# One encoder layer on one core: the column blocks of the input projection in another order

## The chip, the cores and the metric

One core of a Trainium2 chip runs the kernel. The metric is the device time of one execution in microseconds: 886.13 us, median of three runs (884.5 to 888.79). Float32 products are made of three matmuls each: every operand is split into a rounded high part (hi) and a remainder (lo), and hi x hi, hi x lo and lo x hi are summed in PSUM.

## The reference

The input is 2048 tokens of 1024 features. After a LayerNorm one projection gives the columns of three mixers, whose gated outputs are joined and projected back:

```
x = layer_norm(x)
au, av, ag, ba, bb, bg, cq, ck, cv, cg = split(x @ w_in)      # 256,256,256 | 256,256,256 | 512,128,128,512
ya = gelu(au) * (w_s mixed over chunks of 128 tokens of layer_norm(gelu(av)) + b_s) * silu(ag)
yb = silu(layer_norm(depthwise_conv31(ba * sigmoid(bb)) + conv_b)) * silu(bg)
yc = window_attention(cq, ck, cv; +-128 tokens, bias, sink) * silu(cg)
y  = concat(ya, yb, yc) @ w_out
out = layer_norm(alpha * x + y)
```

## The kernel before

The tokens are 16 tiles of 128, in four chunks (NC = 4) of 512. The kernel has three phases. First, x is normalised and transposed into four tiles xc0 to xc3 (one for each chunk, 1024 features by 512 tokens, hi and lo), and the columns av, ck and cv are projected. Second, eighteen blocks of 128 columns are projected, one chunk at a time: 72 steps. A list named plan gives the blocks' order; ft_n_c in the rows is block n of the plan and chunk c. A step is `feat` (24 matmuls into a PSUM tile ft, L139 to L141) and `evac`, which takes the tile away by the kind of the column. Third, block by block of 128 tokens, come scores, softmax, transposes of p, the product with v, the gate and the output projection (`slot`); the first of these slots are put among the last eight steps, from tail0 = 64 on, by a table.

What `evac` does: a conv input bb goes through a sigmoid on ScalarE into glu, and ba is multiplied with it on VectorE (L461). A gMLP column au goes through gelu on ScalarE (L466), then VectorE multiplies it with the spatially mixed tile spT (L468); the matching ag goes through silu (L475), GpSimd multiplies (L478), and `store_y` makes a cast on ScalarE (L433), a remainder on GpSimd (L434) and two stores. A query block cq is split into hi (ScalarE) and lo (VectorE, L232) and stored. A conv gate bg is silu, a GpSimd product and `store_y`; an attention gate cg is silu and one store. ScalarE loads a table (ACT_TABLE_LOAD) when it turns between gelu, silu and exp.

Around these steps hang other pieces of work, tied to step numbers by `at(s, ...)`: the depthwise convolution, 62 operations over 2048 tokens on VectorE ("taps": L382 for the first of each half, L386 for the rest), of which `conv_step` issues so many per step; `vln_tile`, the gMLP's LayerNorm; `conv_ln_tile` and `conv_back`, the conv's LayerNorm with its transposes cl (L407) and cb (L424), two tiles per step from cl0 = 48; and `split_wo`, which loads a piece of w_out, splits it with a ScalarE cast and a GpSimd subtraction (L555) and stores both halves, since there is no room to keep them.

PSUM tiles come from four pairs of buffers, psA, psB, psD and psE. A step's tile is in psD; in psE for every other step of kinds cq and cg. psA holds spT, the transposes of p and, here, cl; psB the transposes cb and the product with v; psD also the scores; psE also the output projection. SyncE issues all DMAs in the order of its queue, and each engine works through its own queue in order. A scheduler chooses how the engines' instructions interleave, so an engine's order is not the order of the code.

Of the kernel before, what the change touches and what calls it, by code (L numbers as in the profile page):

```python
# [7 lines left out]
F32 = mybir.dt.float32  # L8
# [6 lines left out]
P = 128  # L15
# [5 lines left out]
NC = SEQ // CH  # L21
# [15 lines left out]
AU, AV, AG = 0, 256, 512  # L37
BA, BB, BG = 768, 1024, 1280
CQ, CK, CV, CG = 1536, 2048, 2176, 2304
# [16 lines left out]
def trunk_kernel(  # L56
# [42 lines left out]
    psp = tc.alloc_tile_pool(name="psp", bufs=2, space=PSUM)  # L99
# [3 lines left out]
    def rstd_of(pool, var, tag, scale=1.0):  # L103
        ve = pool.tile([P, 1], F32, tag=tag + "e", name=tag + "e", bufs=3)
        G.tensor_scalar(out=ve, in0=var, scalar1=scale, scalar2=EPS, op0=ALU.mult, op1=ALU.add)  # L105
        rs = pool.tile([P, 1], F32, tag=tag + "r", name=tag + "r", bufs=3)
        G.tensor_tensor(out=rs, in0=ve, in1=nhalf, op=ALU.pow)
        return rs

    def stats(pool, srcs, tag, stag=None):  # L110
        stag = stag or tag + "s"
        st = pool.tile([P, len(srcs), 6], F32, tag=stag, name=stag, bufs=2)
        for j, s in enumerate(srcs):
            V.bn_stats(out=st[:, j, :], in_=s)
        mv = pool.tile([P, 2], F32, tag=tag + "m", name=tag + "m", bufs=3)
        V.bn_aggr(out=mv, in_=st)  # L116
        return mv
# [16 lines left out]
    def feat(w, c, name, o=0, n=CH, tag="psD"):  # L134
        ps = psp.tile([P, n], F32, tag=tag, name="ft_" + name)
        hi, lo = w
        for k in range(NK):
            xh, xl = xc[c][:, 0, k, o:o + n], xc[c][:, 1, k, o:o + n]
            T.matmul(ps, hi[:, k, :], xh, start=(k == 0), stop=False)  # L139
            T.matmul(ps, hi[:, k, :], xl, start=False, stop=False)  # L140
            T.matmul(ps, lo[:, k, :], xh, start=False, stop=(k == NK - 1))  # L141
        return ps
# [22 lines left out]
    ps = psp.tile([NH, 512], F32, tag="psE", name="ps_tb")  # L165
# [96 lines left out]
    for t in range(NT + LOOK):  # L262
# [25 lines left out]
        if u >= 2 * TPC and u % TPC == 3:  # L288
# [1 line left out]
    keys(NC - 1, 0, CH)  # L290
    values(NC - 1, 0, CH)

    plan = [(BB, "bb", 0), (BA, "ba", 0), (BB + P, "bb", 1), (BA + P, "ba", 1),
            (AU, "au", 0), (AG, "ag", 0), (AU + P, "au", 1), (AG + P, "ag", 1)]
    plan += [(CQ + a * P, "cq", a) for a in range(4)]
    plan += [(CG + a * P, "cg", a) for a in range(2)]
    plan += [(BG + a * P, "bg", a) for a in range(2)]
    plan += [(CG + a * P, "cg", a) for a in range(2, 4)]
    wts = {}

    def want(n):
        if n < len(plan) and n not in wts:
            wts[n] = prep_w(plan[n][0], f"f{n}")
# [30 lines left out]
    def prep_spatial():  # L334
        SY.dma_start(vgb[:, 0, :], gmlp_ln_g[0].partition_broadcast(P))
        SY.dma_start(vgb[:, 1, :], gmlp_ln_b[0].partition_broadcast(P))
        wsr = pm.tile([P, 4, P], F32, tag="tmp", name="wsr")
        SY.dma_start(wsr, w_spatial[0].rearrange("h i j -> i h j"))
        SY.dma_start(bsp, b_spatial[0].rearrange("h i -> i h"))
        ps = psp.tile([P, 4 * P], F32, tag="psE", name="ps_wt")  # L340
        for h in range(4):
            T.transpose(ps[:, h * P:(h + 1) * P], wsr[:, h, :], ident)
        S.copy(wth, ps)
        V.tensor_tensor(out=wtl, in0=ps, in1=f32(wth), op=ALU.subtract)
# [17 lines left out]
    def spatial(g):  # L362
        vh, vl = vsp.pop(g)
        so = [pm.tile([P, 2, 256], F32, tag="tmp", name=f"so{g}_{j}") for j in range(2)]
        for h in range(4):
            ps = psp.tile([P, TPC, HD], F32, tag="psE", name=f"sp{g}_{h}")
            fs = slice(h * HD, (h + 1) * HD)
            cs = slice(h * P, (h + 1) * P)
            T.matmul(ps, wth[:, cs], vh[:, :, fs], start=True, stop=False)
            T.matmul(ps, wth[:, cs], vl[:, :, fs], start=False, stop=False)  # L370
            T.matmul(ps, wtl[:, cs], vh[:, :, fs], start=False, stop=True)
            for j in range(2):
                S.activation(so[j][:, :, fs], ps[:, 2 * j:2 * j + 2, :], AF.Identity, bias=bsp[:, h:h + 1])
        for j in range(2):
            r0 = (g * TPC + 2 * j) * P
            SY.dma_start(spo_d[r0:r0 + 2 * P, :].rearrange("(c p) f -> p c f", p=P), so[j])
# [17 lines left out]
    def conv_step(n):  # L394
        for _ in range(n):
            if avail[0] <= 0:
                return
            avail[0] -= 1
            next(conv)
# [2 lines left out]
    pbs = {}  # L402

    def conv_ln_tile(t):
        ps = psp.tile([P, 256], F32, tag="psA", name=f"cl{t}")
        for a in range(2):
            T.transpose(ps[:, a * P:(a + 1) * P], acc[a][:, t * P:(t + 1) * P], ident)  # L407
        mv = stats(pm, [ps], "ns")
        rs = rstd_of(pm, mv[:, 1:2], "ns")
        cn = pm.tile([P, 256], F32, tag="cn", name=f"cn{t}")  # L410
        V.tensor_scalar(out=cn, in0=ps, scalar1=mv[:, 0:1], scalar2=rs,
                        op0=ALU.subtract, op1=ALU.mult)
        cns[t] = cn
# [28 lines left out]
    def mixed(a, c):  # L442
        sp = pm.tile([P, TPC, P], F32, tag="ug", name=f"spo{a}_{c}")
        SY.dma_start(sp, spo_d[c * CH:(c + 1) * CH, a * P:(a + 1) * P].rearrange("(b p) f -> p b f", p=P))
        pt = psp.tile([P, CH], F32, tag="psA", name=f"spT{a}_{c}")
        for j in range(TPC):
            T.transpose(pt[:, j * P:(j + 1) * P], sp[:, j, :], ident)
        spt[a, c] = pt
# [40 lines left out]
    def load_k():  # L489
        for j, src in ((0, kh_d), (1, kl_d)):  # L490
            for kv in range(2):
                tkt = pm.tile([P, SEQ], F32R, tag="glu" if kv == 0 else "acc", name=f"k{j}{kv}")
                for o in range(2):
                    SY.dma_start(f32(tkt[o * HD:(o + 1) * HD, :]), src[kv * HD:(kv + 1) * HD, :])
                kt.append(tkt)
# [37 lines left out]
    def open_f32r():  # L533
        t = xtp.tile([P, 2 * NK * CH], F32R, tag="xc1", name="arena1")
        ar["ph"] = [t[:, j * 512:(j + 1) * 512] for j in range(4)]
        ar["pl"] = [t[:, (4 + j) * 512:(5 + j) * 512] for j in range(4)]
        ar["oh"] = [t[:, (8 + j) * 512:(9 + j) * 512] for j in range(2)]
        ar["ol"] = [t[:, (10 + j) * 512:(11 + j) * 512] for j in range(2)]
        ar["v"] = [t[:, 6144 + j * 256:6144 + (j + 1) * 256].rearrange("p (a d) -> p a d", a=2)
                   for j in range(8)]  # L540
# [252 lines left out]
    def at(s, fn, *args):  # L793
        hooks.setdefault(s, []).append((fn, args))

    steps = []
    for n in range(4):
        steps += [(n, c) for c in range(NC)]
    for n in (4, 6):
        for c in range(NC):  # L800
            steps += [(n, c), (n + 1, c)]
    for n in range(8, 16):
        steps += [(n, c) for c in range(NC)]
    tail0 = len(steps)
    for c in range(NC):
# [7 lines left out]
        at(cl0 + t // 2, conv_ln_tile, t)  # L813
        at(cl0 + t // 2 + 1, conv_back, t)
    for j in range(16):
        at(33 + j, split_wo, j % 8, j // 8)
    prep_spatial()

    taps = 0.0
    for s, (n, c) in enumerate(steps):  # L820
        want(n)
        if c == 0:
            want(n + 1)
        if c == 1:
            want(n + 2)
        kind = plan[n][1]
        if s in (6, 9, 12, 15):
            spatial((6, 9, 12, 15).index(s))
        if kind == "au":
            mixed(plan[n][2], c)  # L830
        ps = feat(wts[n], c, f"{n}_{c}", tag="psE" if kind in ("cq", "cg") and s % 2 else "psD")
        evac(kind, plan[n][2], c, ps)
        for fn, args in sorted(hooks.get(s, []), key=lambda e: e[0] is vln_tile or e[0] is conv_ln_tile):
            fn(*args)
        if s == cl0 - 1:
            conv_step(2 * KW)
        elif s >= 8:
            taps += 1.0 if s < 12 else 1.75
            if s < 12:
                with tc.issue_after(anchor["v"]):  # L840
                    conv_step(int(taps))
            else:
                conv_step(int(taps))
            taps -= int(taps)
        r = s - tail0
        if r == 0:
            load_k()
        if r == 1:
            open_f32()
        if r == 3:  # L850
            open_f32r()
            load_v(0)
            load_v(1)
        if r == 5:
            open_wo(0)
        for h in range(SLOTS[max(r, 0)], SLOTS[max(r + 1, 0)]):
            slot(h // 8, h % 8)
# [40 lines left out]
```

## Time and profile before

| | |
|---|---|
| median of three runs | 886.13 us |
| profiled execution | 885.97 us, of which span 884.2 us |
| PE busy | 834.3 us (94%) |
| VectorE / ScalarE / GpSimd busy | 568.4 / 353.6 / 393.3 us |
| DMA, mean over the span | 148 GB/s |
| granted TensorE clock, mean | 0.987 |

The span is what the profile covers, from the first to the last instruction. An engine's busy time counts its instructions without waits. The granted clock is a share of 2.4 GHz. In the rows below a tile's name stands without its number, so ft is any step's tile.

### The profile page before, as it was taken

What the parts mean: (1) busy time and instruction counts of PE and PEld (TensorE: products, weight loads), DVE (VectorE), ACT (ScalarE), POOL (GpSimd) and SP (SyncE); (2) the same over time, 40 slices, a digit from 0 to 9 for tenths busy, and PEclk for the clock granted to TensorE, in tenths of its full rate; (3) what the DMA queues carried; (4) which work ended last, traced back from release to release, by engine and by line L of the source; (5) the groups of instructions that cost most, each with busy time, mean ns of one, the idle gap of its engine ahead of it and who ended that gap; (6) DMA issues with size and microseconds to landing.
All of it is one profiled execution on the core that took longest, in us unless ns stands there. A gap on an engine that the chain in (4) does not pass through costs nothing.

```text
span 884.2 us, 12071 instructions
## 1 busy us (share of the span) xinstructions
PE 834.3 (94%) x4248; PEld 701.7 (79%) x4248; DVE 568.4 (64%) x954; ACT 353.6 (40%) x764; POOL 393.3 (44%) x374
## 2 busy tenths in 40 slices
PE   3989999999988989999799999999999999999996
PEld 2889888888876777878678887788788888888875
DVE  5798613466999999991133000568677887777764
ACT  2654222222333313222312222875566555566440
POOL 4542111331346636643432452014566666566664
PEclk9999999999999999999989999999999999999999
DMA  6777523222312212579731758987745445433221
GB/s 210 259 255 252 183 87 95 84 83 72 96 48 83 85 47 71 191 250 300 271 98 51 198 177 200 237 337 216 183 120 144 114 113 155 138 108 96 84 77 67
DMA packets 115865, 131.24 MB, mean 148 GB/s; under 512 B 8692, under 2 KB 87059, under 8 KB 115260
## 3 DMA queue, kind: packets, MB, share of 16 engines
q1 hardware_dynamic: 115804, 130.47, 47.9%
q8 instruction: 33, 0.54, 0.3%
q14 instruction: 28, 0.23, 0.1%
HBM read 75.90 MB, written 55.07 MB: 148 GB/s over the span
## 4 chain that ended last, share of the span: by engine, by line
PE 32%; POOL 7%; DMA 6%; DVE 6%; ACT 2%; issue 2%; SPq 1%; POOLq 0%; DVEq 0%; ACTq 0%
PE ft L139 4%; PE ft L140 4%; PE ft L141 4%; PE out L700 3%; PE out L702 3%; PE out L701 3%; PE pt L655 3%; POOL arena L647 2%; PE s L622 2%; PE pv L672 2%; PE pv L673 2%; POOL arena L687 2%; DMA wol_d<-wol 1%; DVE r L737 1%; DMA ql_d<-slo 1%
## 5 line engine op out<-in xcount | busy, mean ns | idle before, releaser
L139 PE MATMUL ft<-xc,hi_f 128*128 128x512 f32 x576 | 229.7, 399 | 11.9 <-ACT gu L466 7.5
L140 PE MATMUL ft<-xc,hi_f 128*128 128x512 f32 x576 | 227.1, 394 | 0.0
L141 PE MATMUL ft<-xc,lo_f 128*128 128x512 f32 x576 | 226.8, 394 | 0.0
L386 DVE SCALAR_TENSOR_TENSOR acc<-glu,cw,acc 128x2048 f32<-128x2048 f32 x60 | 171.2, 2889 | 0.4
L139 PEld LDWEIGHTS ft<-xc,hi_f 128*128 128x128 f32 x576 | 109.7, 190 | 38.2 <-ACT gu L466 9.2
L141 PEld LDWEIGHTS ft<-xc,lo_f 128*128 128x128 f32 x576 | 109.7, 190 | 23.3
L140 PEld LDWEIGHTS ft<-xc,hi_f 128*128 128x128 f32 x576 | 109.6, 190 | 21.8
L625 DVE CUSTOM_DVE_ANT_0 arena<-s,arena,nsink 128x288 f32<-128x288 f32 (+4 forms) x128 | 62.7, 493 | 80.1 <-DMA arena<-qh_d 62.1
L131 POOL TENSOR_TENSOR lo_f<-raw_f,hi_f 128x1024 fp32r<-128x1024 f32 x18 | 57.6, 3201 | 73.4 <-ACT hi_f L129 73.4
L638 ACT ACTIVATE arena<-arena,smg 128x288 f32<-128x288 f32 (+4 forms) x128 | 67.5, 528 | 56.9 <-DVE smg L625 55.6
L685 POOL TENSOR_TENSOR arena<-arena,gt 128x512 f32<-128x512 f32 x16 | 20.6, 1287 | 119.4 <-DVE arena L678 86.1
L660 DVE TENSOR_TENSOR arena<-pt,arena 128x512 fp32r<-128x512 f32 x92 | 62.8, 685 | 14.0 <-ACT arena L659 13.9
L659 ACT CAST arena<-pt 128x512 fp32r<-128x512 f32 x92 | 53.1, 581 | 29.9 <-PE pt L655 29.3
L655 PE MATMUL pt<-ident,arena 128*128 128x128 f32 x368 | 55.9, 274 | 4.8 <-DVE arena L660 4.8
L622 PEld LDWEIGHTS s<-k,q 128*128 128x128 f32 x256 | 46.7, 188 | 13.0 <-DVE smg L625 1.5
L622 PE MATMUL s<-k,q 128*128 128x288 f32 (+4 forms) x256 | 54.3, 296 | 1.3 <-ACT cg L475 0.7
L647 POOL TENSOR_SCALAR arena<-arena,sml 128x288 f32<-128x288 f32 (+2 forms) x104 | 50.1, 501 | 6.3 <-ACT bot L676 4.3
L700 PE MATMUL out<-wo,yh 128*128 128x512 f32 x124 | 51.0, 412 | 0.0
L655 PEld LDWEIGHTS pt<-ident,arena 128*128 128x128 f32 x368 | 43.9, 140 | 8.8 <-issue 4.5
L105 POOL TENSOR_SCALAR nse<-nsm 128x1 f32<-128x1 f32 x48 | 12.3, 257 | 85.5 <-DVE nsm L116 83.0
L700 PE MATMUL out<-wo,arena 128*128 128x512 f32 x124 | 48.9, 394 | 0.0
L701 PE MATMUL out<-wo,yh 128*128 128x512 f32 x124 | 48.7, 393 | 0.0
(167 smaller groups left out, 1669.4 us busy)
## 6 DMA issues: line engine op xcount, KB each, us to landing
raw_f<-in_w_in_dram SPq DMA_DIRECT2D x18, 512.0 KB, 4.2
xhat_d<-x SPq DMA_DIRECT2D x16, 512.0 KB, 5.5
r<-xhat_d SPq DMA_DIRECT2D x16, 512.0 KB, 3.7
x<-in_x_dram SPq DMA_DIRECT2D x15, 512.0 KB, 5.1
out_dram<-r SPq DMA_DIRECT2D x15, 512.0 KB, 3.2
yh_d<-shi SPq DMA_DIRECT2D x16, 256.0 KB, 2.1
yl_d<-slo SPq DMA_DIRECT2D x16, 256.0 KB, 2.3
qh_d<-shi SPq DMA_DIRECT2D x16, 256.0 KB, 3.4
```

The costliest lines, as they stand in the source:

```text
L139: T.matmul(ps, hi[:, k, :], xh, start=(k == 0), stop=False)
L140: T.matmul(ps, hi[:, k, :], xl, start=False, stop=False)
L141: T.matmul(ps, lo[:, k, :], xh, start=False, stop=(k == NK - 1))
L386: V.scalar_tensor_tensor(out=acc[a], in0=glu[a][:, k:k + SEQ], scalar=cw[:, a, k:k + 1], in1=acc[a], op0=ALU.mult, op1=ALU.add)
L622: T.matmul(ps[:, 0:n], d["q"][:, h, :], kt[e * 2 + kv][:, g0:g0 + n], start=(e == 0), stop=(e == 1))
L625: V.tensor_tensor_reduce(out=s[:, k0:k1], in0=ps[:, 0:n], in1=ar["bias"][:, kv, b0:b0 + n], scale=1.0, scalar=nsink[:, h:h + 1], op0=ALU.a ...
L638: S.activation(p, p, AF.Exp, bias=d["g"][:, h:h + 1], scale=-1.0, accum_out=d["l"][:, h:h + 1])
L647: (V if i < 3 else G).tensor_scalar(out=p, in0=p, scalar1=d["l"][:, h:h + 1], scalar2=1.0, op0=ALU.mult, op1=ALU.mult)
L655: T.transpose(ps[:, r, :], d["p"][kv * 4 + r][:, f0:f0 + P], ident)
L660: V.tensor_tensor(out=pl, in0=pf, in1=f32(ph), op=ALU.subtract)
L700: T.matmul(ps, hi, wh, start=(k == 0), stop=False)
L701: T.matmul(ps, hi, wl, start=False, stop=False)
```

## The change

The list of blocks is put in another order: conv inputs (unchanged), the four attention gates cg, the four query blocks, the first gMLP half (au and ag alternating), the conv gates bg, and in the tail, with the first attention slots, the second gMLP half where the last two attention gates were. The rate at which taps are issued follows: 1 per step in steps 8 to 15, 1.9 in 16 to 31, 1.5 after. The transposes cl go to psE. The sixteen calls of `split_wo` move from steps 33 to 48 to steps 0 to 15.

```diff
--- before.py
+++ after.py
@@ -290,12 +290,12 @@
     keys(NC - 1, 0, CH)
     values(NC - 1, 0, CH)
 
-    plan = [(BB, "bb", 0), (BA, "ba", 0), (BB + P, "bb", 1), (BA + P, "ba", 1),
-            (AU, "au", 0), (AG, "ag", 0), (AU + P, "au", 1), (AG + P, "ag", 1)]
+    plan = [(BB, "bb", 0), (BA, "ba", 0), (BB + P, "bb", 1), (BA + P, "ba", 1)]
+    plan += [(CG + a * P, "cg", a) for a in range(4)]
     plan += [(CQ + a * P, "cq", a) for a in range(4)]
-    plan += [(CG + a * P, "cg", a) for a in range(2)]
+    plan += [(AU, "au", 0), (AG, "ag", 0)]
     plan += [(BG + a * P, "bg", a) for a in range(2)]
-    plan += [(CG + a * P, "cg", a) for a in range(2, 4)]
+    plan += [(AU + P, "au", 1), (AG + P, "ag", 1)]
     wts = {}
 
     def want(n):
@@ -402,7 +402,7 @@
     pbs = {}
 
     def conv_ln_tile(t):
-        ps = psp.tile([P, 256], F32, tag="psA", name=f"cl{t}")
+        ps = psp.tile([P, 256], F32, tag="psE", name=f"cl{t}")
         for a in range(2):
             T.transpose(ps[:, a * P:(a + 1) * P], acc[a][:, t * P:(t + 1) * P], ident)
         mv = stats(pm, [ps], "ns")
@@ -794,12 +794,11 @@
         hooks.setdefault(s, []).append((fn, args))
 
     steps = []
-    for n in range(4):
+    for n in range(12):
         steps += [(n, c) for c in range(NC)]
-    for n in (4, 6):
-        for c in range(NC):
-            steps += [(n, c), (n + 1, c)]
-    for n in range(8, 16):
+    for c in range(NC):
+        steps += [(12, c), (13, c)]
+    for n in range(14, 16):
         steps += [(n, c) for c in range(NC)]
     tail0 = len(steps)
     for c in range(NC):
@@ -813,7 +812,7 @@
         at(cl0 + t // 2, conv_ln_tile, t)
         at(cl0 + t // 2 + 1, conv_back, t)
     for j in range(16):
-        at(33 + j, split_wo, j % 8, j // 8)
+        at(j, split_wo, j % 8, j // 8)
     prep_spatial()
 
     taps = 0.0
@@ -835,7 +834,7 @@
         if s == cl0 - 1:
             conv_step(2 * KW)
         elif s >= 8:
-            taps += 1.0 if s < 12 else 1.75
+            taps += 1.0 if s < 16 else 1.9 if s < 32 else 1.5
             if s < 12:
                 with tc.issue_after(anchor["v"]):
                     conv_step(int(taps))
```

The scheduler's order shows three places. The first is VectorE's queue where the first query remainder (slo from ft_8_0, L232) comes, with taps (L386, on the two accumulators acc) around it. Before:

```order
L468 TENSOR_TENSOR gu1_2_2731<-spT1_2_2701,gu1_2_2731 128x512
L386 SCALAR_TENSOR_TENSOR acc0_1891<-glu0_1453,cw_1395,acc0_1891 128x2048
L386 SCALAR_TENSOR_TENSOR acc1_2697<-glu1_1873,cw_1395,acc1_2697 128x2048
L386 SCALAR_TENSOR_TENSOR acc0_1891<-glu0_1453,cw_1395,acc0_1891 128x2048
L386 SCALAR_TENSOR_TENSOR acc1_2697<-glu1_1873,cw_1395,acc1_2697 128x2048
L386 SCALAR_TENSOR_TENSOR acc0_1891<-glu0_1453,cw_1395,acc0_1891 128x2048
L468 TENSOR_TENSOR gu1_3_2803<-spT1_3_2773,gu1_3_2803 128x512
L386 SCALAR_TENSOR_TENSOR acc1_2697<-glu1_1873,cw_1395,acc1_2697 128x2048 x3
L232 SCALAR_TENSOR_TENSOR slo_2870<-ft_8_0_2844,shi_2869 128x512
L386 SCALAR_TENSOR_TENSOR acc1_2697<-glu1_1873,cw_1395,acc1_2697 128x2048 x2
L232 SCALAR_TENSOR_TENSOR slo_2908<-ft_8_1_2882,shi_2907 128x512
```

After:

```order
L386 SCALAR_TENSOR_TENSOR acc0_1967<-glu0_1453,cw_1395,acc0_1967 128x2048
L232 SCALAR_TENSOR_TENSOR slo_2901<-ft_8_0_2875,shi_2900 128x512
L386 SCALAR_TENSOR_TENSOR acc0_1967<-glu0_1453,cw_1395,acc0_1967 128x2048
L386 SCALAR_TENSOR_TENSOR acc1_2777<-glu1_1941,cw_1395,acc1_2777 128x2048
L386 SCALAR_TENSOR_TENSOR acc0_1967<-glu0_1453,cw_1395,acc0_1967 128x2048
L232 SCALAR_TENSOR_TENSOR slo_2939<-ft_8_1_2913,shi_2938 128x512
L386 SCALAR_TENSOR_TENSOR acc1_2777<-glu1_1941,cw_1395,acc1_2777 128x2048
L232 SCALAR_TENSOR_TENSOR slo_2972<-ft_8_2_2946,shi_2971 128x512
L386 SCALAR_TENSOR_TENSOR acc1_2777<-glu1_1941,cw_1395,acc1_2777 128x2048 x3
L232 SCALAR_TENSOR_TENSOR slo_3004<-ft_8_3_2978,shi_3003 128x512
```

Before, multiplications of the gMLP half (L468) stand between the taps ahead of the query remainder, and from the last L461 to it there are eight of them; now only taps do. In both the remainders that follow stand one to three taps apart.

The second is GpSimd's queue where the conv's LayerNorm begins (nse, nsr: the 1/sqrt of its first tile; wol: a weight remainder of split_wo; lo_f: the remainder of a column block). Before:

```order
L555 TENSOR_TENSOR wol4_1_3428<-wor4_1_3424,woh4_1_3427 128x512
L555 TENSOR_TENSOR wol5_1_3469<-wor5_1_3465,woh5_1_3468 128x512
L131 TENSOR_TENSOR lo_f14_3581<-raw_f14_3577,hi_f14_3579 128x1024
L555 TENSOR_TENSOR wol6_1_3509<-wor6_1_3505,woh6_1_3508 128x512
L555 TENSOR_TENSOR wol7_1_3546<-wor7_1_3542,woh7_1_3545 128x512
L105 TENSOR_SCALAR nse_3558<-nsm_3556 128x1
L107 TENSOR_TENSOR nsr_3560<-nse_3558,nhalf_80 128x1
```

After:

```order
L131 TENSOR_TENSOR lo_f11_3047<-raw_f11_3043,hi_f11_3045 128x1024
L131 TENSOR_TENSOR lo_f12_3183<-raw_f12_3179,hi_f12_3181 128x1024
L131 TENSOR_TENSOR lo_f13_3319<-raw_f13_3315,hi_f13_3317 128x1024
L131 TENSOR_TENSOR lo_f14_3484<-raw_f14_3480,hi_f14_3482 128x1024
L105 TENSOR_SCALAR nse_3461<-nsm_3459 128x1
L107 TENSOR_TENSOR nsr_3463<-nse_3461,nhalf_80 128x1
```

The weight remainders no longer stand ahead of the LayerNorm's first tile; the product L478 and remainder of the first gMLP half now follow after four of its tiles.

The third is the tail, ScalarE's queue first (q0: cast queries of block 0; arena with smg: exps of its scores; shi: cast of a product). Before:

```order
L588 CAST q0_4436<-arena0_4369 128x512 x2
L475 ACTIVATE cg3_1_4428<-ft_17_1_4403 128x512
L638 ACT_TABLE_LOAD
L638 ACTIVATE arena0_4369,sml0_4441<-arena0_4369,smg0_4440 128x160
L638 ACTIVATE arena0_4369,sml0_4441<-arena0_4369,smg0_4440 128x192
L638 ACTIVATE arena0_4369,sml0_4441<-arena0_4369,smg0_4440 128x224
L638 ACTIVATE arena0_4369,sml0_4441<-arena0_4369,smg0_4440 128x256
L640 ACTIVATE sme0_4439<-sme0_4439 128x4
L638 ACTIVATE arena0_4369,sml0_4441<-arena0_4369,smg0_4440 128x160
L475 ACT_TABLE_LOAD
L475 ACTIVATE cg2_2_4499<-ft_16_2_4474 128x512
L638 ACT_TABLE_LOAD
```

After:

```order
L475 ACTIVATE ag1_0_4321<-ft_17_0_4296 128x512
L433 CAST shi_4324<-gu1_0_4281 128x512
L466 ACT_TABLE_LOAD
L466 ACTIVATE gu1_1_4368<-ft_16_1_4343 128x512
L588 CAST q0_4410<-arena0_4330 128x512 x2
L475 ACT_TABLE_LOAD
L475 ACTIVATE ag1_1_4396<-ft_17_1_4371 128x512
L638 ACT_TABLE_LOAD
L638 ACTIVATE arena0_4330,sml0_4415<-arena0_4330,smg0_4414 128x160
L433 CAST shi_4399<-gu1_1_4368 128x512
L638 ACTIVATE arena0_4330,sml0_4415<-arena0_4330,smg0_4414 128x192
L638 ACTIVATE arena0_4330,sml0_4415<-arena0_4330,smg0_4414 128x224
```

Where there was one silu there are now a gelu and a silu with a table load each and a cast, on both sides of q0. SyncE's queue at the same place (qh_d, ql_d: the stored queries of a block; rep_d: the bias). Before:

```order
L484 DMA g_d_70<-cg3_0_4366 128x512
L531 DMA arena0_4369<-rep_d_74 32x2x288 x3
L584 DMA arena0_4369<-qh_d_65 64x8x128
L484 DMA g_d_70<-cg2_1_4400 128x512
L585 DMA arena0_4369<-ql_d_66 64x8x128
L584 DMA arena0_4369<-qh_d_65 64x8x128
```

After:

```order
L444 DMA spo1_2_4448<-spo_d_62 128x4x128
L531 DMA arena0_4330<-rep_d_74 32x2x288 x4
L584 DMA arena0_4330<-qh_d_65 64x8x128
L435 DMA yh_d_63<-shi_4324 128x512
L436 DMA yl_d_64<-slo_4325 128x512
L585 DMA arena0_4330<-ql_d_66 64x8x128
L584 DMA arena0_4330<-qh_d_65 64x8x128
```

The stores of a gMLP product (yh_d, yl_d) now stand between the two loads of block 0's queries, where the store of a gate stood.

## Rows read from the trace of the kernel before

**Rows 1.** Stages, all engines (start:end, length, busy time and count of PE, PEld, DVE, ACT, POOL, clock, DMA).

```profile
228.10:335.80 107.70, 97.25 (x415) 78.27 (x413) 107.66 (x46) 36.55 (x41) 54.23 (x18) 0.95 0.23 71
431.30:483.80 52.50, 46.71 (x224) 38.59 (x223) 15.66 (x44) 12.65 (x20) 18.86 (x33) 0.93 0.33 113
528.50:596.50 68.00, 66.78 (x328) 54.91 (x327) 28.30 (x97) 40.46 (x89) 9.20 (x5) 1.00 0.88 255
...
393.10:431.30 38.20, 38.20 (x168) 31.59 (x169) 8.66 (x9) 9.97 (x16) 12.97 (x9) 1.00 0.84 280
```

**Rows 2.** Waits of PE (engine, line, awaited: us, times, longest).

```profile
PE ft L139 <- ACT gu L466: 7.5, 5, 2.3
PE cb L424 <- DVE cn L411: 5.8, 2, 5.6
...
PE ft L139 <- ACT ag L475: 2.9, 1, 2.9
...
PE ft L139 <- DVE slo L232: 1.3, 1, 1.3
```

**Rows 3.** Stretches at half clock, columns as in Rows 1.

```profile
266.60:270.00 3.40, 3.40 (x10) 2.63 (x9) 3.40 (x3) 0.56 (x1) 1.14 (x1) 0.51 0.50 154
...
321.20:324.60 3.40, 3.40 (x9) 2.62 (x9) 3.40 (x2) 1.56 (x2) 0.38 (x1) 0.51 0.46 153
440.70:447.50 6.80, 4.30 (x14) 3.41 (x15) 2.71 (x7) 0.00 (x0) 3.40 (x9) 0.50 0.64 196
```

**Rows 4.** Timeline of ScalarE (start, duration, engine, line, [idle before, releaser]).

```profile
262.72 0.62 ACT L433 CAST shi<-gu 128x512 fp32r<-128x512 f32 x1 [9.52 <-POOL gu L478]
263.36 1.28 ACT L466 ACT_TABLE_LOAD   x1
264.65 0.60 ACT L466 ACTIVATE gu<-ft 128x512 f32<-128x512 f32 x1
```

**Rows 5.** Timeline of VectorE at four places.

```profile
231.65 0.68 DVE L461 TENSOR_TENSOR glu<-ft,glu 128x512 f32<-128x512 f32 x1
...
300.85 11.18 DVE L386 SCALAR_TENSOR_TENSOR acc<-glu,cw,acc 128x2048 f32<-128x2048 f32 x4
...
328.78 15.57 DVE L386 SCALAR_TENSOR_TENSOR acc<-glu,cw,acc 128x2048 f32<-128x2048 f32 x5
344.27 0.68 DVE L468 TENSOR_TENSOR gu<-spT,gu 128x512 f32<-128x512 f32 x1
344.88 2.33 DVE L386 SCALAR_TENSOR_TENSOR acc<-glu,cw,acc 128x2048 f32<-128x2048 f32 x1
```

**Rows 6.** Timeline of GpSimd beside two of these.

```profile
301.07 3.26 POOL L478 TENSOR_TENSOR gu<-ag,gu 128x512 f32<-128x512 f32 x1 [5.16 <-DVE gu L468]
305.06 2.55 POOL L434 TENSOR_TENSOR slo<-gu,shi 128x512 fp32r<-128x512 f32 x1 [0.73 <-ACT shi L433]
...
335.50 4.44 POOL L131 TENSOR_TENSOR lo_f<-raw_f,hi_f 128x1024 fp32r<-128x1024 f32 x1
```

**Rows 7.** Timeline of GpSimd, VectorE and PE at the conv LayerNorm's start.

```profile
440.19 1.26 POOL L555 TENSOR_TENSOR wol<-wor,woh 128x512 fp32r<-128x512 f32 x1 [2.99 <-DMA wol_d<-wol]
...
442.39 0.55 DVE L411 TENSOR_SCALAR cn<-cl,nsm,nsr 128x256 f32<-128x256 f32 x1 [6.67 <-POOL nsr L107]
...
442.99 0.69 PE L424 MATMUL cb<-ident,cn 128*128 128x128 f32 x2 [5.57 <-DVE cn L411]
```

**Rows 8.** VectorE's taps as one group (busy, mean ns, idle before).

```profile
L386 DVE SCALAR_TENSOR_TENSOR acc<-glu,cw,acc 128x2048 f32<-128x2048 f32 x60 | 171.2, 2889 | 0.4
```

**Rows 9.** Timelines of GpSimd, SyncE's queue and ScalarE in the tail.

```profile
539.54 3.95 POOL L519 MEMSET arena<- 128x4608 f32 x1 [6.85 <-PE ft L141]
...
546.01 0.59 SPq L585 DMA_DIRECT2D arena<-ql_d  x1
...
550.07 1.14 ACT L588 CAST q<-arena 128x512 fp32r<-128x512 f32 x2 [4.46 <-DMA arena<-ql_d]
```

**Rows 10.** DMA issues of one kind (count, KB each, median us to landing).

```profile
wo<-woh_d SPq DMA_DIRECT2D x8, 512.0 KB, 6.2
```

## The prediction

> **What bounds the kernel now.** I read the row of busy shares first, then the PE waits, then the table by stage, then timelines at the places that these name. TensorE (PE) is busy 94% of the span; what can be won or lost is its idle time and the stretches in which its clock is halved. By stage [rows 1]: from 228.1 to 335.8 us (the sixteen steps in which the gMLP's u and gate columns alternate) PE is busy 97.25 of 107.70 us; the first steps of the conv LayerNorm, 431.3 to 483.8, have 46.71 of 52.50; the tail with the first attention slots, 528.5 to 596.5, 66.78 of 68.00. The last row of the group is a stretch without a gap: 168 matmuls in 38.20 us, 0.2274 us each, so a step of 24 is 5.46 us.
>
> The waits say who holds PE up [rows 2]: 7.5 us in five waits for the gelu and 2.9 in one for the gate's silu, 5.8 for the conv LayerNorm's normalised tile, 1.3 for a query remainder. After such gaps the granted clock is 0.5, which is the 1.2 GHz level [rows 3]: three stretches of 3.40 us beside the gMLP steps (the first and the last are shown), each behind a gap of over 2.3 us with PE busy throughout, and one of 6.80 at the conv LayerNorm with PE busy 4.30 of it. Work at half speed loses half its time: 3 x 1.7 = 5.1 and 2.2 us.
>
> **What goes.** In the gMLP steps ScalarE stands for 9.52 us in front of the cast of the previous product, because that product on GpSimd waits for VectorE's multiplication (L468), which is queued behind conv taps; gelu, with its table load, is behind the cast [rows 4]. The change puts the gates, which need ScalarE alone, where these steps were, and the gMLP halves where no taps are left. So 10.4 + 5.1 go. At the conv LayerNorm, GpSimd's 1/sqrt lies behind a weight remainder (L555) that has to wait 2.99 us for a store to give a buffer back; VectorE stands 6.67 us and PE 5.57 [rows 7]. With the weights split in steps 0 to 15 nothing of that kind is ahead of it: 5.8 + 2.2. The 1.3 at the first query is replaced by a larger one below, and the tail's own 68.00 - 66.78 = 1.2 by the tail's new sum. Together 26.2 us, and the profiled 885.97 becomes 859.8. (885.97 is the span 884.2 and 1.77 around it, 0.16 below the median 886.13 of the three runs.)
>
> **What comes: the queries.** Steps 32 on still store a remainder on VectorE (L232), and the order puts the first behind 41 conv operations counted from the last GLU product (L461 of ft_3_3), which stood at 231.65 [rows 5]. In the changed kernel eight of the weight remainders fall on steps 8 to 15, beside the early taps. A 128x512 operation of GpSimd beside a tap costs it 1.03: four taps with two such take 11.18, and alone one is 2.33, each starting 0.06 or so before the row of the former ends, so 2.27 [rows 5, 6]. Half of the eight beside taps is 4 us; I put that product at 235.5 (232 to 237). A 128x1024 weight remainder (L131) costs a tap 2.1: 15.57 for five, less 5 x 2.27 and 2 x 1.03. Between the product and the first query remainder lie 40 taps and one first tap (92.1 with its 1.3 above a plain one, an estimate from the same rows), two weight remainders of the split (2.1) and five L131 (10.5), and its own 0.7: done at 340.9. PE gets to the step that needs its buffer, the fifth query step, at 228.1 + 20 x 5.46 = 337.3. Wait 3.6, with semaphores 4; the next odd and even steps follow at 1.9 and 0.8, since three taps (6.8) lie between two remainders where a step is 5.46. One half-clock stretch: 1.7. Sum 8.4. Lowest if the product is at 232: 2.5. Highest if each of the 40 taps takes the mean of all, 2.889 [rows 8]: 40 x 0.62 = 25 against the 12.6 of contention counted, 12 more, 20.8. I take 8.4, since the mean comes from a stage with three GpSimd operations per gMLP step, which are no longer there.
>
> **The gMLP half beside the conv LayerNorm (steps 48 to 55).** VectorE has no taps there, so L468 runs at once. New beside it are table loads of 1.28 [rows 4] between gelu and the conv's silu. ScalarE was busy 12.65 of 52.50 us there [rows 1]; the eight loads are 10.3 and eight gelus and silus 4.8, so it stays near half. The LayerNorm's transposes move from psA to psE, which no projection of this stage uses then; psA holds the spatial tiles. I take 1.5, from 0 to 3. The weights' split in steps 0 to 15 puts 16 casts, 16 GpSimd operations and 32 stores into queues of a stage in which PE has no wait; I take 0.8, from 0 to 4 (a late transfer shifting a step once).
>
> **The tail (64 to 71), where the sum decides.** Before, gate columns of conv output need one silu each, and half their tiles lie in psE. Now each pair needs gelu, silu, two products, a cast, a remainder and two stores, all eight tiles lie in psD, which the scores use too, and psA holds spatial tiles beside the transposes of p. Three places, in time from the tail's start W = 528.5:
> First, the scores of block 0. GpSimd's clearing of the score frames (3.95, ends at W + 15.0) was followed by nothing [rows 9]; now the product of the gMLP (1.3), cast (0.62) and remainder (1.3) come behind it, and SyncE has the store of that remainder ahead of the load of q's low half. The load, issued at W + 17.5 and landed 4.06 later, goes to about W + 19, the casts (1.14) end at W + 24.3, and the silu of ag1_1, which frees a psD tile for the third score, is behind them and a table load: W + 26.2. Four feats and two transposed tiles end at W + 22.4; five scores on one tile at a time put ft_16_2 at W + 27.4 where 24.1 would do: 3.3.
> Second, behind ft_16_2 (ends W + 32.9): table load, gelu, table load, three exps with read-outs (1.4), e, two casts of q1 (1.1, as for q0 [rows 9]): 1.28 + 0.60 + 1.28 + 1.4 + 0.2 + 1.1 = 5.9 before block 1's first score. PE has three scores and eight transposes of p to do meanwhile, 1.8. Idle 4.1; one clock stretch, 1.7. Before, ft_17_2 in psE was cut up between these.
> Third, the out projection's first weight, 3.9 us after ft_17_2 at best and 6.2 in the median [rows 10], now stands ahead of ft_16_3 on PE; some 3.7 of other work is ahead of it: 0 to 3, I take 1.5.
> So 8.9 + 1.7 = 10.6. From below, 2 (all three covered by reordered waits); from above, 23.6: 3.3 and then for each of the five steps from ft_17_1 on a wait and a clock stretch as beside the gMLP before, 2.35 + 1.7.
> The Trainium skill ("ScalarE: Activation LUTs", What ACT_TABLE_LOAD costs) has a drain of about 1.38 us with each switch, 2.66 in all. Rows 4 don't show it: the gelu starts 0.01 us after its load ends. By the rule the four switches on the tail's chain would cost 5.5 more, and the sum would be near 887.
>
> **Sum.** 859.8 + 8.4 + 1.5 + 0.8 + 10.6 = 881.1: 881.
>
> **Rivals.**
> 1. The waits are covered: the first GLU product comes at 232 and the tail's scores find tiles free. 859.8 + 2.5 + 0 + 0 + 2 is 864; I say 865. For it: before, PE loses 1.2 us in a tail that has table switches as well. Against it: the tiles of the pairs were in two pools there.
> 2. The tail costs more than it gives, so the whole is slower: one psD pair for scores and gMLP halves makes each of five steps wait for ScalarE's switching, at the upper price. 870.5 before the tail, plus 23.6: 894. It decides from a loss of 20 us in the tail, twice what I sum. For it: the same alternation of gelu and silu is what PE waited for most before, and exp is a third table. Against it: no taps hold VectorE here.
> 3. The taps are late by their mean: 881.1 + 12.4 = 893.5, slower too, with a wait of about 16 us at the fifth query step.
> 4. Switches with a drain (the page's rule), 887: little for it in rows.
>
> **How the numbers follow.** About 0.5% (4.4 us) can be told from no change, so faster means below 881.7 and slower above 890.6. Forecast 0.60, from 874 to 889 by its terms: 0.33 of it faster, 0.26 the same, 0.01 slower. Rival 1 0.14, faster. Rival 2 0.17 and rival 3 0.05, slower. Rival 4 0.04, the same. In all 0.47, 0.30, 0.23. For 8 in 10 I go from 869, which leaves out most of rival 1, to 893, about half of rival 2.
>
> **What would show it.** Right: no PE wait for gelu or silu between 228 and 316 and clock 1.00 there; the cb wait under 1 us; a new wait for slo (L232) of some 4 us near 337, with two small ones behind; PE gaps before s0_0, s1_0 and around out0_0 of 10 us in all. Wrong: waits for gu in steps 48 to 55 (then it wasn't the taps that held L468), a first slo before 338, or PE idle for more than 20 us in the tail.

## The result and the profile after

The changed kernel takes 898.29 us (median of four runs, 896.31 to 899.76), 1.0132 times the kernel before (95% interval 1.0099 to 1.0164). The kernel before took 886.29 us beside it, so the changed one is slower by 12 us, where 881 was forecast, with 893 as the upper end. The profiled execution took 897.57 us, span 895.8. In two of the experiments below, e1 and e2, some executions took 16 to 20 us longer than the others (922.24 and 922.59 beside 902.64 and 905.53 us; 910.5 to 912.32 beside 891.81 and 894.13), so their ratios and profiles are those of the shorter ones, and what lengthens the rest is not shown.

The stages answer to [rows 1]. First three stages of the kernel before, cut at the same steps as the changed kernel's below (from the first step to step 16, steps 32 to 47, and steps 48 to 55), with the columns of that group:

```profile
132.60:228.20 95.60, 95.60 (x448) 78.85 (x446) 52.47 (x104) 26.96 (x67) 25.87 (x36) 1.00 0.28 83
335.80:425.90 90.10, 88.64 (x385) 71.83 (x386) 65.50 (x34) 22.46 (x34) 45.62 (x20) 1.00 0.63 214
425.90:484.30 58.40, 52.61 (x253) 43.54 (x252) 15.84 (x44) 13.75 (x21) 19.93 (x34) 0.94 0.38 130
```

Then the changed kernel: first step to step 16, gates (16 to 31), queries (32 to 47), first gMLP half with the conv LayerNorm (48 to 55), the tail's first 72 us:

```profile
130.20:236.80 106.60, 98.19 (x443) 79.57 (x442) 58.85 (x104) 34.75 (x80) 47.83 (x50) 0.97 0.54 171
236.80:323.80 87.00, 87.00 (x385) 72.06 (x384) 86.97 (x36) 14.85 (x22) 40.09 (x7) 1.00 0.26 87
323.80:430.00 106.20, 90.16 (x390) 74.07 (x389) 63.35 (x37) 14.01 (x22) 32.01 (x5) 0.92 0.32 109
430.00:481.70 51.70, 51.70 (x266) 43.46 (x264) 17.35 (x47) 22.87 (x27) 22.74 (x36) 1.00 0.26 82
527.90:600.00 72.10, 64.76 (x295) 51.54 (x294) 22.13 (x76) 38.47 (x78) 16.73 (x11) 0.95 0.73 203
```

The gate steps and the conv LayerNorm have no idle PE time, as forecast. Two other stages are longer: the first by 11.0 us, the queries by 16.1. PE's waits name both (answering to [rows 2]; the wait for `gu` and `ag` at the feature steps is gone, that for `cn` fell from 5.8 to 1.2):

```profile
PE ft L139 <- ACT cg L475: 16.0, 1, 16.0
...
PE sp L369 <- ACT so L373: 7.8, 3, 6.8
...
PE s L622 <- ACT q L588: 2.8, 2, 1.9
...
PE cb L424 <- DVE cn L411: 1.2, 1, 1.2
```

The wait of 16.0 is for the silu of a gate, at the third query step. The timelines of GpSimd, VectorE, SyncE's queue, ScalarE and PE there:

```profile
303.24 41.95 POOL L131 TENSOR_TENSOR lo_f<-raw_f,hi_f 128x1024 fp32r<-128x1024 f32 x1 [18.96 <-ACT hi_f L129]
...
259.44 83.55 DVE L386 SCALAR_TENSOR_TENSOR acc<-glu,cw,acc 128x2048 f32<-128x2048 f32 x35
352.90 0.69 DVE L232 SCALAR_TENSOR_TENSOR slo<-ft,shi 128x512 fp32r<-128x512 f32 x1 [9.91 <-issue]
...
286.64 17.36 SPq L484 DMA_DIRECT2D g_d<-cg  x4
345.21 0.38 SPq L127 DMA_DIRECT2D raw_f<-in_w_in_dram  x1
345.69 6.97 SPq L484 DMA_DIRECT2D g_d<-cg  x4
...
350.28 0.60 ACT L475 ACTIVATE cg<-ft 128x512 f32<-128x512 f32 x1 [36.46 <-DMA g_d<-cg]
...
350.93 0.80 PE L139 MATMUL ft<-xc,hi_f 128*128 128x512 f32 x1 [16.04 <-ACT cg L475]
```

A weight remainder on GpSimd that took 4.44 us beside taps in [rows 6] takes 41.95. It ends 2.2 us after the last of a row of taps that follow each other without anything between (259.44 + 83.55 = 342.99; the 35 in the line are those from 259.44 on, and the whole row has 41, from 244.29). The next load of weights (raw_f, L127) waits for it in SyncE's queue; the gates' stores stand behind that load, so ScalarE has no free tile for its next silu for 36.46 us, so the step's PSUM tile stays occupied, and PE stands. VectorE's own lag, on which the prediction had put its wait, was not what PE met: the taps are through at 343, and VectorE then stands for 9.91 us before the first query remainder.

In the first stage ScalarE waits for a piece of w_out whose load was issued at 207.63, and the spatial tiles' evacuation (so, L373) is behind that cast in its queue:

```profile
207.63 0.39 SPq L546 DMA_DIRECT2D wor<-in_w_out_dram  x1
...
210.79 0.62 ACT L554 CAST woh<-wor 128x512 fp32r<-128x512 f32 x1 [5.01 <-DMA wor<-in_w_out_dram]
211.31 0.59 ACT L459 ACTIVATE glu<-ft 128x512 f32<-128x512 f32 x1
211.81 1.14 ACT L373 ACTIVATE so<-sp,bsp 128x128 f32<-128x128 f32 x4
...
212.48 0.58 PE L369 MATMUL sp<-vh,sparena 128*128 128x256 f32 x1 [6.78 <-ACT so L373]
```

### The profile page after: what moved, and what is told of

The parts are those of the page before. It is cut to its first block, busy times and chain, and to the rows that moved or that the text cites. A ratio compares the mean times of both kernels' runs of the same rounds, so it can differ in the third digit from the quotient of the medians.

```text
span 895.8 us, 12040 instructions
## 1 busy us (share of the span) xinstructions
PE 833.1 (93%) x4248; PEld 699.6 (78%) x4248; DVE 559.4 (62%) x954; ACT 348.9 (39%) x760; POOL 404.0 (45%) x374
## 4 chain that ended last, share of the span: by engine, by line
PE 53%; POOL 15%; DMA 10%; DVE 9%; issue 6%; ACT 4%; SPq 1%; POOLq 0%; DVEq 0%; ACTq 0%
PE ft L139 9%; PE ft L140 9%; PE ft L141 9%; POOL lo_f L131 5%; PE out L700 3%; PE out L702 3%; PE out L701 3%; PE pt L655 3%; DMA wor<-in_w_out_dram 2%; PE s L622 2%; POOL arena L647 2%; PE pv L672 2%; PE pv L673 2%; DMA x<-in_x_dram 1%; POOL slo L434 1%
## 5 line engine op out<-in xcount | busy, mean ns | idle before, releaser
L140 PE MATMUL ft<-xc,hi_f 128*128 128x512 f32 x576 | 226.3, 393 | 0.0
L131 POOL TENSOR_TENSOR lo_f<-raw_f,hi_f 128x1024 fp32r<-128x1024 f32 x18 | 89.9, 4996 | 164.6 <-ACT hi_f L129 164.6
L386 DVE SCALAR_TENSOR_TENSOR acc<-glu,cw,acc 128x2048 f32<-128x2048 f32 x60 | 153.2, 2603 | 0.2
L702 PE MATMUL out<-wo,yl 128*128 128x512 f32 x124 | 49.0, 395 | 0.0
```

The costliest lines, as they stand in the source:

```text
L131: G.tensor_tensor(out=lo, in0=raw, in1=f32(hi), op=ALU.subtract)
L386: V.scalar_tensor_tensor(out=acc[a], in0=glu[a][:, k:k + SEQ], scalar=cw[:, a, k:k + 1], in1=acc[a], op0=ALU.mult, op1=ALU.add)
L702: T.matmul(ps, lo, wh, start=False, stop=(k == NK - 1))
```

## The experiments

The theory after the result: (A) an unbroken row of taps can keep GpSimd out until the row is interrupted, and through SyncE's in-order queue and ScalarE's this becomes PE's wait; (B) the early split costs the first stage its 11 us; (C) the tail's gaps come from the tiles that gMLP halves and scores share. The rivals are in the expectations. Each edit is to the changed kernel unless it says otherwise. The kernel before ran beside each set: 884.28 us for the first four, 884.84 for the next four, 884.89 for the last two. That is some 2 us less than the 886.29 beside the changed kernel, so a difference from the changed kernel is also given by the ratios to the kernel before.

**e1: the weights split late.**

```diff
-        at(j, split_wo, j % 8, j // 8)
+        at(33 + j, split_wo, j % 8, j // 8)
```

> The changed kernel with the weights split in steps 33 to 48 again, as before the change; all else as changed. Theory A (the early split holds ScalarE, GpSimd and SyncE's queue beside the gMLP LayerNorm, so the mixed tiles come late): the stage from the first projected step to step 16 takes 95 to 97 us where the changed kernel's profile has 106.6, and the conv LayerNorm's first tile waits 5 to 6 us again with a half-clock stretch. If the wait of 16 us at the third query step stays: about 895; if GpSimd's long weight remainder falls on another moment and is not held: about 878. Theory B (the early stage was late for another reason, such as the taps' new rate): the stage stays at 104 or more, and the whole is at 900 or above.

The first stage took 95.1 us (131.2 to 226.3): B holds. The whole was slower than the changed kernel, 1.0218 times the kernel before (1.0176 to 1.0259), because the hold came earlier and lasted longer:

```profile
270.97 57.87 POOL L131 TENSOR_TENSOR lo_f<-raw_f,hi_f 128x1024 fp32r<-128x1024 f32 x1 [18.88 <-ACT hi_f L129]
```

PE then waited 32.2 us for a gate. The case of a longer hold I had not listed. Nor did the conv LayerNorm's first tile wait 5 to 6 us again, as A had it: PE's wait for `cn` is 1.1 us, with the weights split as late as in the kernel before.

**e2: the gates' stores issued from ScalarE's queue.**

```diff
-                SY.dma_start(g_d[a * P:(a + 1) * P, cs], tm)
+                S.dma_start(g_d[a * P:(a + 1) * P, cs], tm)
```

> The changed kernel with the stores of the attention gates issued from ScalarE's queue and not from SyncE's. Theory A (GpSimd's weight remainder is held for 42 us, SyncE's queue stands at the weight load that needs its buffer, and the gates' stores behind it keep the silu's tiles occupied, so ScalarE and then PE stand): GpSimd's remainder still takes about 42 us, but the PE wait of 16.0 us for the gate's silu is under 1.5 us, a wait of 0 to 4 us for the first query remainder or for the weights' remainder takes its place, and the time is 880 to 885. Theory B (the taps as such are late, by my prediction's step): the wait stays at 14 us or more and the time at 896 to 900.

Ratio 1.0089 (1.0051 to 1.0127), 891.81 us in the profiled execution, and not 880 to 885. The hold was there (41.91 us), and PE's wait fell to 10.3 us, not under 1.5. The rest has a second path that I had overlooked: the same weight load holds up the cast of the weights, which stands in ScalarE's queue ahead of the last silu.

```profile
350.02 1.04 ACT L129 CAST hi_f<-raw_f 128x1024 fp32r<-128x1024 f32 x1 [29.87 <-DMA raw_f<-in_w_in_dram]
350.97 0.59 ACT L475 ACTIVATE cg<-ft 128x512 f32<-128x512 f32 x1
```

So the stores account for 5.7 of the 16.0 us. The theory of late taps, which foretold no change, falls.

**e3: a break behind every third tap.**

```diff
                                       op0=ALU.mult, op1=ALU.add)
+                if k % 3 == 0:
+                    V.memset(glu[a][:, 0:PAD], 0.0)
                 yield
```

> The changed kernel with a clearing of the 15 padding columns of glu (already zero, so no value changes) behind every third tap, which puts a VectorE instruction that reads nothing from SBUF into the unbroken row of 35 taps; the longest row is then 7. Theory A (GpSimd is held as long as the taps follow each other without a break): no weight remainder takes more than 18 us (7 taps), the wait of 16 us is under 4, the time 882 to 887. Rival A2 (a break of 0.1 us is too short for GpSimd to take its turn, or the hold is no matter of breaks): one remainder still takes over 30 us, and the time is 897 to 901.

885.41 us, ratio 1.0017 (1.0002 to 1.0032), 12.9 us less than the changed kernel or, by the ratios, 10. No remainder is held, and what is left of the wait is the one that the prediction had worked out, for the query remainders, 4.6 us in three (forecast: 4, 1.9 and 0.8, together 6.7):

```profile
303.09 3.88 POOL L131 TENSOR_TENSOR lo_f<-raw_f,hi_f 128x1024 fp32r<-128x1024 f32 x1 [18.77 <-ACT hi_f L129]
324.85 2.49 POOL L131 TENSOR_TENSOR lo_f<-raw_f,hi_f 128x1024 fp32r<-128x1024 f32 x1 [17.88 <-ACT hi_f L129]
...
PE ft L139 <- DVE slo L232: 4.6, 3, 2.6
```

This alone doesn't show that breaks end a hold: they also shift the moments at which GpSimd starts, and here none was held at all.

**e4: every other tile of the tail in psE.**

```diff
-        ps = feat(wts[n], c, f"{n}_{c}", tag="psE" if kind in ("cq", "cg") and s % 2 else "psD")
+        ps = feat(wts[n], c, f"{n}_{c}", tag="psE" if (kind in ("cq", "cg") or s >= tail0) and s % 2 else "psD")
```

> The changed kernel with every other step's tile of the tail in psE, as the steps of kinds cq and cg have it, so that the gMLP halves leave psD to the scores half of the time. Theory A (the tail's gaps come from the tiles shared with the scores): PE's gaps from 528 to 600 fall from 7.3 us to 3 or less, and the time by 4 to 6, to 892 to 894. Theory B (ScalarE's switching between three tables, and the late queries behind the product's store, make them): the gaps stay at 6 us or more and the time within 2 us of 898.

889.78 us, ratio 1.006 (1.0032 to 1.0089), 8.5 less than the changed kernel or, by the ratios, 6.4. From the tail's start to the end it takes 360.3 us where the changed kernel takes 367.9 and the kernel before 355.7. The gaps fell from 7.3 to 4.4, less than forecast, and the clock's 0.95 in that stretch rose to 1.00:

```profile
527.40:600.00 72.60, 68.20 (x343) 56.09 (x342) 29.96 (x102) 44.65 (x95) 16.80 (x11) 1.00 0.82 245
```

So C holds for some two thirds of the tail's loss (7.6 of 12.2 us). Of the remaining 4.6, sixteen transposes of spatial tiles that the new order puts into the tail are some 1.8 (an estimate from 0.11 us between two of them in the trace); the rest fits the table switches and the late queries, which I didn't test apart.

**e5: one break, behind the 31st tap after the second half's first.**

```diff
                                       op0=ALU.mult, op1=ALU.add)
+                if a == 1 and k == 15:
+                    V.memset(glu[a][:, 0:PAD], 0.0)
                 yield
```

> The changed kernel with one clearing of glu's 15 padding columns (already zero) behind the 31st tap after the second half's first one; up to there VectorE's row is as in the changed kernel, where the remainder that was held 41.95 us started in the 22nd tap. Theory A1 (once held, GpSimd waits until the row of taps is interrupted, however shortly): the remainder starts near 303 and is held again, but ends about 2.25 us behind the break, near 327, so it takes 22 to 26 us; the wait of 16 us at the third query step is under 2, and the time is 881 to 886. Rival A2 (so short a break doesn't let GpSimd in, and the many breaks of the kernel before only shifted the moments at which its operations start): about 42 us again, the wait 14 to 16 us, the time 896 to 900.

886.51 us, a little above the 881 to 886 that were expected, ratio 1.0018 (1.0 to 1.0037). GpSimd and VectorE:

```profile
301.96 23.69 POOL L131 TENSOR_TENSOR lo_f<-raw_f,hi_f 128x1024 fp32r<-128x1024 f32 x1 [19.19 <-ACT hi_f L129]
...
251.27 76.53 DVE L386 SCALAR_TENSOR_TENSOR acc<-glu,cw,acc 128x2048 f32<-128x2048 f32 x30
323.35 0.07 DVE L390 MEMSET glu<- 128x15 f32 x1
327.72 18.06 DVE L386 SCALAR_TENSOR_TENSOR acc<-glu,cw,acc 128x2048 f32<-128x2048 f32 x7
```

The remainder is held again, and ends at 325.65, 2.23 us after the end of the break of 0.07 (the group of 30 goes on over the break, and its last tap, which waited for GpSimd, ends at 327.80). That is what tells the two apart: an interruption of 0.07 us lets GpSimd in. PE's wait for the gate is gone; in its place are 5.7 us in two waits for query remainders.

**e6: breaks and late split.** The edits of e1 and e3.

> The kernel with a break behind every third tap, and the weights split in steps 33 to 48 again. If the early split costs the first stage what it takes longer there (106.6 against 95.1 us in the kernel that only splits late), and the hold is gone with the breaks, the two add up: 885.4 less 11, plus 2 to 4 for the weights' remainders beside the taps of steps 33 to 40: 874 to 880, stage 1 at 95 to 97 us, and a wait of 5 us or more for the conv LayerNorm's first tile is back, or, as in the kernel that only splits late, not. If the rival holds (a late split lets GpSimd be held whatever breaks there are): a remainder of over 20 us and 890 or more.

884.58 us, ratio 1.0003 (0.9981 to 1.0025), so not 874 to 880. The first stage took 95.2 us and nothing was held, but 11 us came back in steps 48 to 55: PE waited 9.0 us for the load of a spatial tile (spT <- spo), which uses the same two buffers (ug) as the weight pieces and stands behind their stores in SyncE's queue. Before, this stage had no spatial tiles.

**e7: e6 with the tail's tiles as in e4.**

> The last kernel with every other tile of the tail in psE as well. The tail's part was worth 8.5 us by itself (898.3 to 889.8); if it adds up, 866 to 871, and faster than the kernel before by 1.5 to 2%. If the tail's waits are made up for by the stage before it (queries later, weights' stores in SyncE's queue), 873 or more.

873.63 us, ratio 0.9871 (0.985 to 0.9891). The time is in the expectation's second case, because the stage before the tail is late, as in e6; the tail's part does add up, since e7 is 11 below e6. The spatial tile's wait, and SyncE's queue, where its load follows the store of a weight remainder, 7.7 us after the step began:

```profile
PE spT L449 <- DMA spo<-spo_d: 11.1, 2, 9.4
...
411.31 0.32 SPq L559 DMA_DIRECT2D wol_d<-wol  x1
411.68 0.43 SPq L446 DMA_DIRECT2D spo<-spo_d  x1
```

**e8: the kernel before with only the split moved to steps 0 to 15.**

> The kernel before with only the weights' split moved to steps 0 to 15. Theory A (its place costs the first stage some 11 us and gives the conv LayerNorm's start 8 back): stage 1 (first step to step 16) 104 to 107 us, cb wait under 2 us, the time 885 to 890. My prediction's step (0.8 lost, 8.0 won): stage 1 at 96 to 97, the time 876 to 879.

893.35 us, ratio 1.0083 (1.0056 to 1.011): 8.5 slower, more than either expected. Its first stage and its conv LayerNorm's start:

```profile
131.40:237.60 106.20, 98.42 (x444) 80.01 (x443) 58.58 (x104) 34.71 (x80) 47.78 (x50) 0.97 0.54 172
439.10:489.30 50.20, 50.20 (x253) 42.12 (x252) 15.15 (x43) 11.44 (x17) 15.10 (x30) 1.00 0.20 69
```

106.2 against 95.6, and the 8 us at the LayerNorm are won, as A has it. The gMLP steps lost some 4 more (a spatial tile came 7.4 us late there), and the tail 2.7.

**e9 and e10: e7 with the split in steps 29 to 44, and in steps 24 to 39.**

> The kernel with breaks and the tail's tiles in psE, with the weights split in steps 29 to 44. In the last one (steps 33 to 48) PE waited 9.4 us for a spatial tile's load at step 48 and the stage of steps 48 to 55 took 63.6 us where an early split has 51.8. Theory A (the last weight pieces hold the buffers and the place in SyncE's queue that the spatial tiles need, and four steps are enough to be clear of it): that wait under 2 us, the stage 51 to 54, and 873.6 less 11 gives 861 to 866. Rival (the load is late whatever the split does, or the pieces beside the taps delay the query remainders by as much): 870 or more.

> The same with the split in steps 24 to 39. Stage of steps 48 to 55 at 51 to 54 as well. Some five more weight remainders lie beside taps, 1.03 each, so the first query remainders come 5 us later: PE waits 5 to 8 us for them in steps 36 to 40 in place of 1.9, and the time is 4 to 6 us above the kernel with the split in 29 to 44: 866 to 871. If the queries do not wait longer, it is the same as that one.

e9: 863.8 us, ratio 0.9759 (0.9734 to 0.9784), the fastest of all. e10: 867.82, ratio 0.9807 (0.9781 to 0.9833). e9 by stage, as above:

```profile
130.50:225.80 95.30, 95.30 (x444) 78.48 (x442) 54.19 (x105) 28.61 (x70) 30.14 (x39) 1.00 0.35 108
225.80:312.80 87.00, 87.00 (x385) 72.14 (x384) 86.84 (x49) 14.15 (x20) 12.16 (x4) 1.00 0.23 76
312.80:404.40 91.60, 88.76 (x389) 72.03 (x389) 65.19 (x41) 19.64 (x31) 42.23 (x17) 1.00 0.60 207
404.40:456.20 51.80, 51.80 (x268) 43.59 (x266) 18.73 (x49) 24.42 (x29) 22.72 (x36) 1.00 0.35 112
```

Three of the four stages have no idle PE time, and the wait for the spatial tile's load, 9.4 us in e7, is 0.9. e10 came out at the time that was foretold but not for the reason: its query remainders make PE wait 3.4 us, against 2.8 in e9, and the first stage is 3.7 us longer (99.0). The traces show why. The scheduler put the pieces that are tied to steps before 32 into the first stage, three in e9 and eight in e10, and the others from 319 us on; so the step numbers of these two edits are not where all of the work ran. In e10 one of the eight casts, at 167.01, waited 6.13 us for its load with the spatial tiles' evacuation behind it, as in B:

```profile
PE sp L369 <- ACT so L373: 2.1, 1, 2.1
```

A half-clock stretch of 3.41 us follows that wait, which loses 1.7 more.

## Why the prediction was wrong

By stages, from the profiled executions; the kernel before runs from 132.6, the changed one from 130.2, where nothing was changed.

| | forecast | measured |
|---|---|---|
| first step to step 16 | +0.8 | +11.0 |
| steps 16 to 31 | -15.5 | -20.6 |
| steps 32 to 47 | +7.1 | +16.1 |
| steps 48 to 55 | -6.5 | -6.7 |
| steps 56 to 63 | 0 | +2.0 |
| tail and rest | +9.4 | +12.2 |

With -2.4 at the start that is 11.6, the difference of the spans. The forecast's terms add up to -4.7 and not to -4.9: what goes is 26.0 us and not 26.2, which makes 881.3 of 881.1.

What was right: the gMLP steps' waits and their clock stretches went, because no tap holds L468 (part of the -20.6 is not saved: the spatial tiles' transposes, some 30 matmul records, went to later stages). The conv LayerNorm's start won what it should; e8 shows that the early split does this in the old order, but in the new one the wait is as short with a late split (1.1 us in e1, 1.2 in e6), so there the early split was not needed for it. The tail lost about what was summed, at the places named: 0.90 and 1.02 us around the first scores, 0.82, 0.38 and 1.90 before block 1's, 0.47 at the out projection, and one of 1.51 for a spatial tile that I hadn't listed; the first term was 3.3 and measured 1.9.

Two steps failed. The larger is the contention in "What comes: the queries". It read from [rows 5, 6] that a GpSimd operation beside taps costs VectorE 1.03 or 2.1 us. In those rows the operation itself was always done a tap later, and a price on VectorE was all I drew from them. But the kernel before never had more than a few taps in a row: a multiplication (L468) or a remainder stood between them. The order of the changed kernel, which I had in front of me, has 41 operations with nothing between, and what that could do to GpSimd I did not ask. The wait came out as 16.0 us for a gate and not 4 for a remainder; with the breaks (e3) the forecast's own three waits appear, 4.6 us for the 6.7 summed. The taps were not late by themselves: from the product to the last of the 41 they took 99.3 us, where the forecast has 104.7.

The other is "I take 0.8, from 0 to 4" for the early split: 11.0 in the changed kernel, 10.6 alone (e8), 0 when it is late (e1, e9). I had argued that PE has no wait in that stage. ScalarE, GpSimd and SyncE's queue all carry the gMLP's LayerNorm there, whose spatial product PE does need, and each piece of w_out puts a load into the middle of that chain: the cast waits 5.01 us for it, and everything behind the cast in ScalarE's queue with it.

The rivals of the slower side named the wrong places. The tail took 3 us more than forecast, not 13. Rival 3, late taps, comes close in numbers, 893.5 us and a wait of about 16 at the fifth query step, but by chance: the 16.0 stand at the third, for a gate, while the taps took less than the forecast gave them.

What stays open: why one start beside a tap is held and another isn't. The held ones started 0.98 to 1.28 us after the beginning of a tap, with GpSimd idle for some 19 us before. But in e2 one that started 1.05 after, with 5.38 idle before, took 3.55 us, and in e9 one that started 1.14 after, with 19.23 idle, took 3.44; there the next boundary was between two taps, but a break had come as the tap that it met began. In the profiles of kernels without regular breaks every remainder that had both was held and no other was; five cases from kernels so much alike don't make that a cause.

## What to carry to other kernels

Moving work off a busy engine's queue also takes out what stood between its long instructions; ask what those gaps gave to the engine that shares memory with it, and look in the order for the longest unbroken row. A break of 0.07 us in such a row was worth 10 to 12 us here (e5). Work that is moved into a stage where PE does not wait should be followed through every in-order queue of that stage (loads, casts, stores) up to the instruction that PE needs next, and through the buffers whose tag it shares. Where a scheduler orders the work, look in the trace where a moved piece ran: a step number in the code did not say it in e9 and e10.

## What the runs showed of the hardware

A GpSimd operation that meets a row of VectorE taps (two inputs and the output in SBUF) normally runs behind the tap in progress, and the next tap waits for it: the remainder ends 2.25 us after that tap, and the tap takes 4.48 instead of 2.34. The Trainium skill ("SBUF — State Buffer", Who interferes with whom) has a VectorE instruction with two SBUF inputs contend with a GpSimd instruction that reads SBUF, and calls the pair of ports that they share an exclusive lock. These rows agree: each of the two waits for the end of the other's instruction. In the held cases the wait went on over many instructions. Four executions that were profiled had one remainder that got in at none of the boundaries between the following taps: 41.95 us in the changed kernel, 41.91 in e2, 57.87 in e1, 41.90 in e4; in e5, with one break, 23.69. Each ended some 2.2 us after the row's end or its break. In the kernels with a break behind every third tap (e3, e6, e7, e9, e10) none took more than 4.6.
